# First norm's gain and shift applied behind the gather, in a decoder layer with 32 experts

## The chip, the cores and the metric

The kernel runs on one core of one Trainium2 chip. The metric is the device time of one execution in microseconds (us), as the median of several runs. A core has TensorE (PE, matmuls; its results go to PSUM), VectorE (DVE), ScalarE (ACT), GpSimd (POOL) and SyncE (SP), which here issues all the DMA transfers, in program order, each as soon as its buffer is free.

## The reference

One decoder layer of width 1024 over 512 tokens. Both norms are layer norms with a gain and a shift for each of the 1024 features:

```python
merged = gates[:, :, 0] * (pool_out @ w_pu[i]) + gates[:, :, 1] * (attn_out @ w_au[i])
x = layer_norm(DEEPNORM_ALPHA * x + merged @ w_o[i], ln1_g[i], ln1_b[i])
moe_out = hierarchical_moe(x, w_rg[i], b_rg[i], w_re[i], b_re[i], w_eg[i], w_eu[i], w_ed[i])
ple = jax.nn.sigmoid(x @ w_pg[i]) * (p[i] @ w_pp[i])
x = layer_norm(DEEPNORM_ALPHA * x + moe_out + ple, ln2_g[i], ln2_b[i])
```

`hierarchical_moe` sends each token to one of 4 groups by the largest of 4 logits and there to the two experts of 8 with the largest logits; an expert is `(silu(x @ w_eg) * (x @ w_eu)) @ w_ed` with 512 inner features. An expert's weights are 6 MB, those of all 32 together 192 MB.

## The kernel before

The tokens lie in four blocks of 128 rows (`tb` 0 to 3). Mixers and attention run first (to about 310 us); then comes `merged @ w_o` in two column halves (`out_proj`), and from its second half on everything around the change, in an order that is written out by hand (`tc.manual_schedule`); each engine works through its own instructions in that order.

**Norm and routing of a block.** `residual` adds alpha times the input and takes the statistics, `moments` and `shift` make the row's factor (with a power on GpSimd), `normalise` applies it on ScalarE (`acc[tb]` is then normalised, without gain and shift). `turn` transposes that into `x1T`, split into a high and a low part (ScalarE copies the high part out of PSUM, VectorE subtracts). `route` makes the logits from it; the gain and the shift are already folded into the router's weights and bias there. `gain`, `offset` and `affine` (L769 to L777) then multiply and add the rows of `ln1_g` and `ln1_b` into `acc[tb]`, each half on VectorE or GpSimd; `keep_high` (ScalarE) and `keep_low` (VectorE or GpSimd) split the result into the two parts of `x1[tb]`. `choose` picks group and experts for two blocks at a time in some 15 small VectorE instructions, `place` makes each token's slot with two or three matmuls, `one_hots` the matrix G that gathers.

**Gather and experts.** The 32 experts are worked on in 12 units of 2 to 4 experts; 128 slots are filled in each. `gather` multiplies x1 by G into PSUM, four banks `kb` 0 to 3 for the eight blocks of 128 features, and `keep_slots` copies them to `xgs`. For the first unit this goes bank by bank, blocks 0 and 1 of the tokens ahead, blocks 2 and 3 once the second choice is done; later units are gathered two at a time beside the experts, with the banks of `zz` (two). `inner` is the first pair of expert matmuls, `outer` the last one. The function `pair(j, ...)` runs one unit; between, `scatter` adds the unit before to `acc`. At the end of its first run `renew` (L894) rebuilds x1 from its two parts into `acc` on VectorE, scaled by alpha on ScalarE. Units 3 and 4 carry the first steps of `embedding`, which transposes x1 again (`split_transpose`) for `x @ w_pg`; it takes buffers out of the stream meanwhile.

**The weight stream.** Weights come in chunks of 1 MB, 192 in all. A chunk's buffer is one of 8 named s8, 6 of the pool wst (wraw, whi, wlo), 2 named more and, once each, 2 named acc. `FIRST` lists the chunks that go out before it is known which experts are busy (three experts are fixed, the rest go by a ranking of token counts that `count_tokens` and `rank` make); `eload_first(n)` issues them up to the nth. All others follow in their order through `eload_past`, each when TensorE has read a chunk and its buffer is free.

Of the kernel before, what the change touches and what calls it, by code (L numbers as in the profile page):

```python
# [20 lines left out]
S, D = 512, 1024  # L21
# [16 lines left out]
def layer_kernel(ctx: ExitStack, tc: tile.TileContext, x, p, w_in, w_pool, pool_scale, w_pu, w_au,  # L38
# [393 lines left out]

    x1, acc = {}, {}
# [16 lines left out]
    g1 = lnt.tile([128, D], F32, name="g1")  # L450
    b1 = lnt.tile([128, D], F32, name="b1")
    nc.sync.dma_start(g1, rows_bcast(ln1_g, D))
    nc.sync.dma_start(b1, rows_bcast(ln1_b, D))
# [60 lines left out]
    def source(i):  # L514
# [4 lines left out]
    FIRST = [(0, "s8"), (1, "s8"), (2, "s8"), (4, "s8"), (5, "wraw"), (6, "whi"), (8, "wlo"), (9, "wraw"), (10, "s8"),  # L519
             (11, "s8"), (12, "s8"), (15, "s8"), (18, "whi"), (21, "wlo"), (3, "acc"), (24, "more"), (27, "more"),  # L520
             (7, "acc")]
# [201 lines left out]
    def relabel(rk, w2):  # L723

        full = [128, 2, NT, E]
        t, u = (lnt.tile(full, F32, name=n, tag=t) for n, t in (("by_rank", "g1"), ("by_slot", "b1")))
# [42 lines left out]
    def gain(tb, h, eng):  # L769
        eng.tensor_mul(acc[tb][:, halves[h]], acc[tb][:, halves[h]], g1[:, halves[h]])  # L770

    def offset(tb, h, eng):
        eng.tensor_add(acc[tb][:, halves[h]], acc[tb][:, halves[h]], b1[:, halves[h]])

    def affine(tb, h, eng):
        gain(tb, h, eng)
        offset(tb, h, eng)  # L777

# [4 lines left out]
    def keep_high(tb):  # L783
        x1[tb] = res.tile([128, 2, D], F32R, name="x1", bufs=4)
        for h in range(2):
            nc.scalar.activation(turned(x1[tb][:, 0], h), acc[tb][:, halves[h]].rearrange("p (m k) -> p m k", k=KD), AF.Copy)
# [7 lines left out]
    eload_first(4)  # L794
# [25 lines left out]
    eload_first(8)  # L820
# [41 lines left out]
    def keep_slots(us, o, kb):  # L862
        o = o.rearrange("p (k e s) -> p k e s", k=2, e=2)
        ks = slice(2 * kb, 2 * kb + 2)
# [29 lines left out]
    def renew(b):  # L894

        new_acc(b)
        for tb in (b, b + 1):
            hi, lo = (x1[tb][:, i].rearrange("p (k m) -> p m k", k=KD).bitcast(F32) for i in range(2))
            nc.vector.tensor_add(acc[tb].rearrange("p (m k) -> p m k", k=KD), hi, lo)  # L899
# [12 lines left out]
    with tc.manual_schedule():  # L912
# [3 lines left out]
        eload_first(9)  # L916
# [8 lines left out]
        eload_first(10)  # L925
        residual(1, 1, o)
        moments(1)
        gain(0, 0, dve)
        shift(1)
        offset(0, 0, dve)  # L930
        affine(0, 1, pool)
# [87 lines left out]
    def pair(j, other, extra):  # L1019
# [19 lines left out]
        for n in range(2):  # L1039
# [14 lines left out]
            if n == 0:  # L1054
                embed(1)
# [330 lines left out]
```

## Time and profile before

| | us |
|---|---|
| median of 3 runs | 873.96 (873.03 to 874.01) |
| the profiled execution | 873.73 |
| its span in the trace | 871.9 |
| PE busy | 805.8 (92%) |
| DVE busy | 412.3 (47%) |
| ACT busy | 214.2 (25%) |
| POOL busy | 191.4 (22%) |

The trace is of one execution; its times count from the span's start. The DMA engines moved 241.89 MB in it, at 277 GB/s over the span; most of that is moved after 340 us. A busy PE need not be PE at its peak, since the ends of matmuls are modelled; whether it waits is read from who releases it, and whether the DMA engines are full from their mean share and rate.

### The profile page before, as it was taken

Reading aid. Unit: us, or ns where it says so; the run is one execution under the profiler, and the core shown is the slowest. Engines: PE = TensorE matmul, PEld = TensorE weight load, DVE = VectorE, ACT = ScalarE, POOL = GpSimd, SP = SyncE. Lnnn points to the kernel's source line nnn. Section 1 sums busy time; section 2 is a strip of 40 time slices with the busy share of each in tenths; the row PEclk is TensorE's granted clock in tenths of the full one; section 3 lists DMA queues with packets and bytes.
Section 4 is the critical chain, followed back from the end, with each engine's and each line's share of the span. In section 5 each row is a group of like instructions: output and inputs, shape, how many; then the busy total and the mean of one; then the engine's idle time right before and its main releaser. Section 6 shows DMA issues by size and latency. Waiting matters only on the chain.

```text
span 871.9 us, 11544 instructions
## 1 busy us (share of the span) xinstructions
PE 805.8 (92%) x4454; PEld 511.5 (59%) x4454; DVE 412.3 (47%) x691; ACT 214.2 (25%) x443; POOL 191.4 (22%) x176
## 2 busy tenths in 40 slices
PE   8999899899999998699999887899799999999983
PEld 7886677677768887635345333566375744545432
DVE  5278647645448858847442432221123244343437
ACT  3123444444461114313101011210220101100214
POOL 3333324224221235600000220231313000000225
PEclk9999999999999999689999989999999999999997
DMA  7431131222213786657999999999999999999992
GB/s 253 140 99 52 48 97 49 63 82 63 83 48 143 247 310 248 266 214 271 407 419 419 416 406 418 414 413 407 418 407 404 404 419 419 419 418 421 412 360 99
DMA packets 65787, 241.89 MB, mean 277 GB/s; under 512 B 12096, under 2 KB 32576, under 8 KB 41408
## 3 DMA queue, kind: packets, MB, share of 16 engines
q1 hardware_dynamic: 65728, 241.10, 71.1%
q8 instruction: 37, 0.61, 0.3%
q14 instruction: 22, 0.18, 0.1%
HBM read 238.99 MB, written 2.10 MB: 276 GB/s over the span
## 4 chain that ended last, share of the span: by engine, by line
PE 50%; DMA 11%; DVE 4%; POOL 2%; issue 1%; ACT 1%; SPq 1%; POOLq 0%; ACTq 0%; DVEq 0%
PE mm L907 18%; PE mm L1115 8%; PE xg_ps L848 6%; DMA ew<-in_w_eu_dram 4%; PE sc_ps L1148 4%; PE mm L143 3%; PE mm L145 3%; PE mm L144 3%; DMA ew<-in_w_ed_dram 3%; DMA pr<-in_p_dram 2%; DMA ew<-in_w_eg_dram 2%; PE pg_ps L144 1%; PE pg_ps L143 1%; PE pg_ps L145 1%; DVE acc L899 1%
## 5 line engine op out<-in xcount | busy, mean ns | idle before, releaser
L907 PE MATMUL mm<-ew,xg 128*32 128x512 f32 (+1 forms) x1088 | 189.5, 621 | 16.8 <-DMA ew<-in_w_eu_dram 11.1
L907 PEld LDWEIGHTS mm<-ew,xg 128*32 128x32 f32 (+1 forms) x1088 | 54.8, 125 | 137.3 <-issue 108.3
L1115 PE MATMUL mm<-ew,hT 128*32 128x512 f32 (+1 forms) x544 | 91.6, 597 | 3.0 <-DMA ew<-in_w_ed_dram 2.1
L132 POOL TENSOR_TENSOR wlo<-wraw,whi 128x1024 fp32r<-128x1024 f32 x23 | 69.1, 3003 | 108.4 <-DVE whi L127 52.5
L143 PE MATMUL mm<-xth,whi 128*128 128x512 f32 x224 | 91.6, 409 | 0.0
L145 PE MATMUL mm<-xth,wlo 128*128 128x512 f32 x224 | 88.6, 396 | 0.0
L144 PE MATMUL mm<-xtl,whi 128*128 128x512 f32 x224 | 88.3, 394 | 0.0
L1053 DVE TENSOR_TENSOR h<-mm,h 128x512 f32<-128x512 f32 x24 | 16.6, 692 | 128.9 <-PE mm L907 71.3
L848 PEld LDWEIGHTS xg_ps<-G,x 128*128 128x128 f32 x448 | 56.0, 198 | 13.6 <-issue 9.0
L848 PE MATMUL xg_ps<-G,x 128*128 128x256 f32 (+1 forms) x448 | 59.0, 290 | 1.2 <-DVE xg L867 1.2
L1149 DVE TENSOR_TENSOR acc<-acc,sc_ps 128x512 f32<-128x512 f32 x88 | 54.7, 681 | 6.6 <-PE sc_ps L1148 6.0
L1115 PEld LDWEIGHTS mm<-ew,hT 128*32 128x32 f32 (+1 forms) x544 | 24.7, 120 | 54.5 <-issue 46.1
L143 PEld LDWEIGHTS mm<-xth,whi 128*128 128x128 f32 x224 | 42.8, 191 | 9.5 <-issue 0.9
L144 PEld LDWEIGHTS mm<-xtl,whi 128*128 128x128 f32 x224 | 43.0, 192 | 8.8 <-issue 0.5
L145 PEld LDWEIGHTS mm<-xth,wlo 128*128 128x128 f32 x224 | 42.7, 190 | 9.3
L127 DVE CAST whi<-wraw 128x2048 fp32r<-128x2048 f32 x22 | 26.9, 1225 | 33.8 <-PE mm L144 16.6
L132 DVE TENSOR_TENSOR wlo<-wraw,whi 128x1024 fp32r<-128x1024 f32 x23 | 40.7, 1770 | 1.0
L1164 POOL TENSOR_TENSOR xf<-x 128x1024 f32<-128x1024 f32 x4 | 9.4, 2376 | 144.5 <-PE mm L907 144.5
L1137 POOL TENSOR_TENSOR accl<-acc,acch 128x512 fp32r<-128x512 f32 x8 | 10.5, 1337 | 137.7 <-ACT acch L1136 137.7
L1148 PE MATMUL sc_ps<-yh,Gt 128*128 128x512 f32 x88 | 37.8, 429 | 1.1 <-DVE sg L1220 1.1
L1220 DVE TENSOR_TENSOR sg<-pg_ps,sg 128x256 f32<-128x256 f32 x16 | 6.8, 425 | 65.4 <-ACT sg L1219 65.4
L144 PE MATMUL pg_ps<-pgl,xT 128*128 128x256 f32 x128 | 36.3, 284 | 0.7 <-POOL pgl L1200 0.7
(270 smaller groups left out, 1355.4 us busy)
## 6 DMA issues: line engine op xcount, KB each, us to landing
ew<-in_w_eg_dram SPq DMA_DIRECT2D x64, 1024.0 KB, 16.6
ew<-in_w_eu_dram SPq DMA_DIRECT2D x64, 1024.0 KB, 14.1
ew<-in_w_ed_dram SPq DMA_DIRECT2D x62, 1024.0 KB, 14.1
wraw<-in_w_in_dram SPq DMA_DIRECT2D x15, 1024.0 KB, 5.6
wraw<-in_w_o_dram SPq DMA_DIRECT2D x4, 1024.0 KB, 5.0
pgr<-in_w_pg_dram SPq DMA_DIRECT2D x4, 1024.0 KB, 17.3
wraw<-in_w_pu_dram SPq DMA_DIRECT2D x2, 1024.0 KB, 5.0
wraw<-in_w_au_dram SPq DMA_DIRECT2D x2, 1024.0 KB, 5.0
```

The source lines that it names most:

```text
L127: nc.vector.tensor_copy(hi, wraw[i])
L132: eng.tensor_sub(lo[:, j], wraw[i][:, j], hi[:, j].bitcast(F32))
L143: nc.tensor.matmul(o, lh, rh, start=start, stop=False)
L144: nc.tensor.matmul(o, lh, rl, start=False, stop=False)
L145: nc.tensor.matmul(o, ll, rh, start=False, stop=stop)
L848: nc.tensor.matmul(o[:, kx * 256:kx * 256 + n], x1[tb][:, i, cs], G[tb // 2][:, tb % 2].rearrange("p u s -> p (u s)"), start=whole and tb ...
L907: nc.tensor.matmul(o[cs], xgs[j][:, k, cs], ew[chunk0[j] + ne * (2 * n + k // 4) + i][:, k % 4], start=k == 0, stop=k == KD - 1)
L1053: nc.vector.tensor_mul(ht, o, ht)
L1115: nc.tensor.matmul(o[cs], hT[:, f, cs], ew[chunk0[j] + ne * (4 + f // 2) + i][:, f % 2, halves[c]], start=f == 0, stop=f == 3)
L1137: nc.gpsimd.tensor_sub(l, acc[tb][:, halves[c]], h.bitcast(F32))
L1148: nc.tensor.matmul(o, Gt[:, tb * 128:(tb + 1) * 128], y[c][i], start=i == 0, stop=i == 1)
L1149: nc.vector.tensor_add(acc[tb][:, cs], acc[tb][:, cs], o)
```

## The change

x1 is kept and gathered as normalised only. Gain and shift are applied three times later on: in `keep_slots`, where the gathered features lie one to a partition, so that gain and shift are columns `gq`, `bq` (ScalarE with scale and bias, VectorE with two scalars, one instruction for 128x128 where there was one for 128x256); in `renew`, a block at a time with the rows `gb1`; and in a new `turn_x1` for the embedding. `gain`, `offset` and `affine` go. `gb1` is an s8 buffer, which goes back to the stream at the end of the second pair; `FIRST` is one chunk shorter (27 is left out). `renew` runs for blocks 0 and 1 where it ran for all four, for block 2 at the end of the first pair and for block 3 inside the second.

```diff
+    gb1 = s8([128, 2, D], F32, "gb1")
+    gq, bq = (slp.tile([128, KD], F32, name=n) for n in ("gq", "bq"))
...
-             (11, "s8"), (12, "s8"), (15, "s8"), (18, "whi"), (21, "wlo"), (3, "acc"), (24, "more"), (27, "more"),
-             (7, "acc")]
+             (11, "s8"), (12, "s8"), (15, "whi"), (18, "wlo"), (3, "acc"), (21, "more"), (24, "more"), (7, "acc")]
...
-        nc.scalar.activation(xgs[us[0]][:, ks], o[:, :, 0], AF.Copy)
-        if len(us) > 1:
-            nc.vector.tensor_copy(xgs[us[1]][:, ks], o[:, :, 1])
+        for i in range(2):
+            k = 2 * kb + i
+            nc.scalar.activation(xgs[us[0]][:, k], o[:, i, 0], AF.Identity, scale=gq[:, k:k + 1], bias=bq[:, k:k + 1])
+            if len(us) > 1:
+                nc.vector.tensor_scalar(xgs[us[1]][:, k], o[:, i, 1], gq[:, k:k + 1], bq[:, k:k + 1], op0=OP.mult,
+                                        op1=OP.add)
...
+        nc.vector.tensor_add(acc[tb].rearrange("p (m k) -> p m k", k=KD), hi, lo)
+        nc.vector.tensor_mul(acc[tb], acc[tb], gb1[:, 0])
+        nc.vector.tensor_add(acc[tb], acc[tb], gb1[:, 1])
+        nc.scalar.activation(acc[tb], acc[tb], AF.Copy, scale=ALPHA)
...
-        turn(2, lambda: shift(3))
-        keep_low(1, 1, pool)
-        eload_first(15)
-        affine(2, 1, pool)
+        place(0)
+        turn(2)
+        keep_high(1, (0,))
+        shift(3)
         normalise(3)
-        place(0)
-        one_hots(G[0], (0,), 0)
-        gain(2, 0, dve)
...
         route(2)
+        keep_high(1, (1,))
+        keep_low(1, 0, pool)
+        keep_low(1, 1, dve)
+        one_hots(G[0], (0,), 0)
         turn(3)
-        offset(2, 0, dve)
-        affine(3, 0, dve)
-        affine(3, 1, pool)
+        keep_high(2)
+        keep_low(2, 0, pool)
         route(3)
...
-        for kb in range(3):
+        for kb in range(2):
             gather(G, xs[kb], kb, (0, 1))
-        keep_high(2)
         keep_high(3)
+        keep_low(2, 1, dve)
         choose(lg2, 2)
-        keep_low(2, 0, pool)
-        keep_low(2, 1, pool)
-        keep_low(3, 1, pool)
-        keep_low(3, 0, dve)
-        eload_first(18)
+        keep_low(3, 0, pool)
         place(2)
-        gather(G, xs[3], 3, (0, 1))
+        keep_low(3, 1, dve)
+        eload_first(17)
+        for kb in range(2, 4):
+            gather(G, xs[kb], kb, (0, 1))
...
+                if j == 1:
+                    renew(3)
...
-            for b in (0, 2):
-                renew(b)
+            renew(0)
+            renew(1)
...
+        if j == 0:
+            renew(2)
+        elif j == 1:
+            free.append("s8")
+            eload_past(done[0])
...
+        def turn_x1(xt, src):
+            for h in range(2):
+                pt = tt("x1T_ps")
+                t = ex.tile([128, 4, 128], F32, name="x1t", tag="pph", bufs=1)
...
+                    nc.vector.tensor_scalar(t[:, i], pt[:, i * 128:(i + 1) * 128], gq[:, k:k + 1], bq[:, k:k + 1],
+                                            op0=OP.mult, op1=OP.add)
+                hi, lo = (xt[:, i, 4 * h:4 * h + 4] for i in range(2))
+                nc.scalar.activation(hi, t, AF.Copy)
+                nc.vector.tensor_sub(lo, t, hi.bitcast(F32))
```

The order on VectorE from the first G to the beginning of the second choice, before (x1T are the transposed copies of block 3, g and b the gain and shift rows; `lg` is the choice's first instruction):

```order
L836 TENSOR_TENSOR G<-iota_c,posm 128x256
L770 TENSOR_TENSOR acc<-acc,g_2339 128x512
L596 TENSOR_TENSOR x1T<-x1T_ps,x1T 128x512 x2
L773 TENSOR_TENSOR acc<-acc,b_2340 128x512
L770 TENSOR_TENSOR acc<-acc,g_2339 128x512
L773 TENSOR_TENSOR acc<-acc,b_2340 128x512
L634 TENSOR_TENSOR lg<-lg_ps,lbias 128x80
```

The same stretch on VectorE after (x_2802 and x_2853 are x1 of blocks 1 and 2, so L782 is `keep_low`):

```order
L764 TENSOR_SCALAR rs<-mv,rs 128x1
L782 TENSOR_TENSOR x_2802<-acc,x_2802 128x64x8
L829 TENSOR_TENSOR G<-iota_c,posm 128x256
L598 TENSOR_TENSOR x1T<-x1T_ps,x1T 128x512 x2
L782 TENSOR_TENSOR x_2853<-acc,x_2853 128x64x8
L636 TENSOR_TENSOR lg<-lg_ps,lbias 128x80
```

Four steps with gain and shift are gone from in front of the choice, and two low parts of the split stand there.

On TensorE around the second placing, before (xg_ps with a number is a bank of the gather; 2826 is the fourth, 2823 the first again, for blocks 2 and 3):

```order
L659 MATMUL pos_ps_2952<-msk_2358,strict_67 128x64
L661 MATMUL pos_ps_2952<-msk_2358,ones_66 128x64 x2
L662 MATMUL pos_ps_2952<-msk_2358,ones_66 128x32
L848 MATMUL xg_ps_2826<-G_2544,x1_2688 128x128 x2
L848 MATMUL xg_ps_2826<-G_2544,x1_2742 128x128 x2
L848 MATMUL xg_ps_2826<-G_2544,x1_2688 128x128 x2
L848 MATMUL xg_ps_2826<-G_2544,x1_2742 128x128 x2
L670 MATMUL ct_ps_2968<-msk_2358,ones_66 128x32 x4
```

And after:

```order
L661 MATMUL pos_ps_2926<-msk_2361,strict_67 128x64
L663 MATMUL pos_ps_2926<-msk_2361,ones_66 128x64 x2
L664 MATMUL pos_ps_2926<-msk_2361,ones_66 128x32
L841 MATMUL xg_ps_2809<-G_2545,x1_2685 128x128 x2
L841 MATMUL xg_ps_2809<-G_2545,x1_2802 128x128 x2
L841 MATMUL xg_ps_2809<-G_2545,x1_2685 128x128 x2
L841 MATMUL xg_ps_2809<-G_2545,x1_2802 128x128 x2
L841 MATMUL xg_ps_2810<-G_2545,x1_2685 128x128 x2
L841 MATMUL xg_ps_2810<-G_2545,x1_2802 128x128 x2
L841 MATMUL xg_ps_2810<-G_2545,x1_2685 128x128 x2
L841 MATMUL xg_ps_2810<-G_2545,x1_2802 128x128 x2
L672 MATMUL ct_ps_2953<-msk_2361,ones_66 128x32 x4
```

The third bank's eight matmuls have moved from ahead of the placing to behind it.

On VectorE in the first pair, from the weights of its slots to the evictions of the next gather, before:

```order
L881 TENSOR_TENSOR Gw<-Gw,comb 128x512
L899 TENSOR_TENSOR acc<-x_2688 128x1024
L899 TENSOR_TENSOR acc<-x_2742 128x1024
L899 TENSOR_TENSOR acc<-x_2924 128x1024
L899 TENSOR_TENSOR acc<-x_2927 128x1024
L867 COPY xg<-xg_ps 128x256 x2
```

And after:

```order
L876 TENSOR_TENSOR Gw<-Gw,comb 128x512
L894 TENSOR_TENSOR acc<-x_2685 128x1024
L895 TENSOR_TENSOR acc<-acc,gb_2339 128x1024
L896 TENSOR_TENSOR acc<-acc,gb_2339 128x1024
L894 TENSOR_TENSOR acc<-x_2802 128x1024
L895 TENSOR_TENSOR acc<-acc,gb_2339 128x1024
L896 TENSOR_TENSOR acc<-acc,gb_2339 128x1024
L861 TENSOR_SCALAR xg<-xg_ps,gq,bq 128x128 x4
```

Two blocks instead of four are rebuilt there, each in three steps; the other two stand behind the pair's last results and inside the second pair.

## Rows read from the trace of the kernel before

**Rows 1.** Windows: engines' busy us (instructions), PE clock, DMA share, GB/s

```profile
760.00:800.00 40.00, 40.00 (x186) 16.94 (x184) 16.37 (x26) 3.76 (x6) 0.00 (x0) 1.00 1.01 419
```

**Rows 2.** Windows of 5 us at the stream's beginning

```profile
410.00:415.00 5.00, 5.00 (x52) 1.48 (x48) 1.82 (x3) 1.11 (x2) 0.00 (x0) 1.00 0.39 120
...
420.00:425.00 5.00, 5.00 (x39) 2.17 (x32) 1.48 (x3) 0.00 (x0) 0.00 (x0) 1.00 1.01 426
```

**Rows 3.** Chain that ended last, its end: start us, us, what

```profile
821.03 10.02 DMA ew<-in_w_eu_dram
...
835.35 8.43 DMA ew<-in_w_ed_dram
...
843.82 5.34 PE mm L1115 x42
```

**Rows 4.** Timeline of SP's queue: first issue behind the prefetched chunks

```profile
379.01 8.39 SPq L536 DMA_DIRECT2D ew<-in_w_eg_dram  x4
```

**Rows 5.** Chain from the second choice to the second pair

```profile
351.11 1.68 DVE acc L770
...
354.07 1.64 DVE acc L773
355.70 1.70 DVE acc L770
...
357.43 1.91 DVE acc L773
359.34 0.16 DVE lg L634
...
363.50 0.24 DVE msk L653
...
364.88 1.79 PE xg_ps L848 x8
...
371.93 3.61 PE mm L907 x8
...
377.11 1.87 PE mm L907 x8
...
409.53 13.87 PE mm L907 x128
```

**Rows 6.** Windows around TensorE's lower clock

```profile
360.00:370.00 10.00, 6.12 (x29) 6.15 (x30) 6.43 (x24) 1.84 (x3) 2.27 (x2) 0.50 0.45 164
...
376.00:378.00 2.00, 2.00 (x13) 1.36 (x14) 0.00 (x0) 0.38 (x1) 0.00 (x0) 0.84 0.00 0
```

**Rows 7.** Timeline of DVE: start us, us, line, operation, tiles

```profile
360.14 0.64 DVE L639 CAST gif<-gi 128x2 f32<-128x2 uint32 x1
...
361.96 1.12 DVE L649 CAST e<-i 128x4 f32<-128x4 uint32 x1
...
363.65 1.03 DVE L789 TENSOR_TENSOR x<-acc,x 128x512 fp32r<-128x512 f32 x1
```

**Rows 8.** Timeline of ACT: logits' copy and the high parts

```profile
351.08 0.27 ACT L613 ACTIVATE lt<-lg_ps 72x128 f32<-72x128 f32 x1
...
355.74 2.05 ACT L786 ACTIVATE x<-acc 128x512 fp32r<-128x512 f32 x2 [0.75 <-DVE acc L773]
```

**Rows 9.** Timeline of POOL: the last low part

```profile
361.53 1.52 POOL L789 TENSOR_TENSOR x<-acc,x 128x512 fp32r<-128x512 f32 x1 [0.79 <-ACT x L786]
```

**Rows 10.** Chain in the first pair: rebuild of x1 and eviction

```profile
393.96 9.68 DVE acc L899 x4
...
404.71 0.28 ACT xg L865
...
405.02 0.44 DVE xg L867
```

**Rows 11.** Groups by shape, 318 to 412 us: busy us, mean ns

```profile
L881 DVE TENSOR_TENSOR Gw<-Gw,comb 128x512 f32<-128x512 f32 x1 | 0.7, 691 | 0.0
```

**Rows 12.** Waits of PE from 420 to 860 us: us in total, times, longest

```profile
PE mm L907 <- DMA ew<-in_w_eu_dram: 11.1, 6, 5.1
```

More of the change, by code (lines that the diff above doesn't have):

```diff
@@ L449, in layer_kernel @@
         nc.sync.dma_start(acc[tb], x2[tb * 128:(tb + 1) * 128])
[L450 to L453, printed above, removed]
+    gb1 = s8([128, 2, D], F32, "gb1")
+    gq, bq = (slp.tile([128, KD], F32, name=n) for n in ("gq", "bq"))
+    for i, (w, t) in enumerate(((ln1_g, gq), (ln1_b, bq))):
+        nc.sync.dma_start(gb1[:, i], rows_bcast(w, D))
+        nc.sync.dma_start(t, w[0].rearrange("(p k) -> p k", p=128))
     wrr = lnt.tile([128, KD, 36], F32, name="wrr")
@@ L725, in relabel @@
         full = [128, 2, NT, E]
-        t, u = (lnt.tile(full, F32, name=n, tag=t) for n, t in (("by_rank", "g1"), ("by_slot", "b1")))
+        t, u = (lnt.tile(full, F32, name=n) for n in ("by_rank", "by_slot"))
         r2, s2 = (lnt.tile([128, 2, NT, 1], F32, name=n) for n in ("r2", "s2"))
@@ L767, in normalise, with keep_high @@
             nc.scalar.activation(acc[tb][:, cs], acc[tb][:, cs], AF.Identity, scale=rs[:, :1], bias=rs[:, 1:])
[L769 to L777, printed above, removed]
     def turned(t, h):
         return t.rearrange("p (k m) -> p m k", k=KD)[:, 64 * h:64 * h + 64]
-    def keep_high(tb):
-        x1[tb] = res.tile([128, 2, D], F32R, name="x1", bufs=4)
-        for h in range(2):
+    def keep_high(tb, hs=(0, 1)):
+        if 0 in hs:
+            x1[tb] = res.tile([128, 2, D], F32R, name="x1", bufs=4)
+        for h in hs:
             nc.scalar.activation(turned(x1[tb][:, 0], h), acc[tb][:, halves[h]].rearrange("p (m k) -> p m k", k=KD), AF.Copy)
@@ L892, in turn_one_hots, with renew @@
         return Gt, ws
[L894 to L899, printed above, removed]
+    def renew(tb):
+        if tb % 2 == 0:
+            new_acc(tb)
+        hi, lo = (x1[tb][:, i].rearrange("p (k m) -> p m k", k=KD).bitcast(F32) for i in range(2))
+        nc.vector.tensor_add(acc[tb].rearrange("p (m k) -> p m k", k=KD), hi, lo)
+        nc.vector.tensor_mul(acc[tb], acc[tb], gb1[:, 0])
+        nc.vector.tensor_add(acc[tb], acc[tb], gb1[:, 1])
+        nc.scalar.activation(acc[tb], acc[tb], AF.Copy, scale=ALPHA)
     def inner(j, n, o, ks):
@@ L924, in layer_kernel @@
         out_proj(1, 1, o, parts, range(6, 8))
-        eload_first(10)
+        eload_first(9)
         residual(1, 1, o)
         moments(1)
-        gain(0, 0, dve)
         shift(1)
-        offset(0, 0, dve)
-        affine(0, 1, pool)
         out_proj(2, 1, o, parts, range(0, 2))
@@ L943, in layer_kernel @@
         out_proj(2, 1, o, parts, range(6, 8))
-        eload_first(11)
+        eload_first(10)
         residual(2, 1, o)
         moments(2)
-        gain(1, 0, dve)
+        keep_low(0, 0, pool)
+        keep_low(0, 1, dve)
         shift(2)
-        offset(1, 0, dve)
-        affine(1, 1, pool)
         out_proj(3, 1, o, parts, range(0, 2))
@@ L1081, in pair @@
         if j == 0:
-            for b in (0, 2):
-                renew(b)
-                for tb in (b, b + 1):
-                    nc.scalar.activation(acc[tb], acc[tb], AF.Copy, scale=ALPHA)
+            renew(0)
+            renew(1)
         embed(3)
@@ L1109, in pair @@
         embed(5)
-        return Gt, [weighted(o[c], ws) for c in range(2)]
+        y = [weighted(o[c], ws) for c in range(2)]
+        if j == 0:
[3 more added lines that the diff above has]
+            eload_past(done[0])
+        return Gt, y
     def outer(j, hT, f, c, o):
@@ L1188, in embedding @@
             xT.append(xt)
-            split_transpose(xt, xf[tb])
+            turn_x1(xt, xf[tb])
             if tb % 2:
```

31 lines of the change are left out of this document (16 added, 15 removed).

## Prediction

> **What bounds the kernel now.** I read the stretches first, then the chain from its end backwards, then the SP queue. From 420 us the DMA engines are full: their share is 1.01, at 419 GB/s between 760 and 800 us [rows 1] and 426 at the start [rows 2], and the last two things that TensorE waits for are expert weights, 10.02 us and 8.43 us; the last weights land at 843.78 us and the rest is a fixed tail [rows 3]. So the end is set by the weight stream: by when it becomes full for good, and by how many chunks of 1 MB are still to come then. A chunk costs 1.0486 MB / 419 GB/s = 2.50 us.
>
> The stream could not be full earlier, for it had no free buffers. All 18 buffers are filled before the experts start; the first chunk behind them goes out at 379.01 us [rows 4], 0.03 us after TensorE has read the first chunks (377.11 + 1.87 us) [rows 5]. It stays so for the whole first pair: between 410 and 415 us the DMA share is still 0.39 [rows 2]. The second pair's 128 matmuls take 13.87 us from 409.53 us [rows 5] and free three chunks after each quarter of them, 3.5 us; the first three come free at 413.0 us. That is faster than 2.50 us a chunk can fill, and from there the stream has no gap. So two numbers decide: how much earlier TensorE gets to that point, and how many chunks are left at it.
>
> What TensorE waits for on the way is the second choice of experts. VectorE does four gain and offset steps in front of it (1.68, 1.64, 1.70 and 1.91 us), starts it at 359.34 us and ends it at 363.74 us; only then can TensorE place and gather [rows 5]. TensorE has been idle and is at half speed by then: eight matmuls of L907 take 3.61 us at 371.93 us and 1.87 us at 377.11 us [rows 5]; the granted clock is 0.50, the 1.2 GHz level, and comes back at about 376.7 us (0.84 over that stretch) [rows 6].
>
> **The change, part by part.**
>
> *One prefetch less.* gb1 takes one of the eight s8 buffers, so 17 chunks go out early and chunk 27 joins the stream. The buffer comes back only at the end of the second pair, when the stream is full anyway. Price: one chunk, **+2.50 us**. Its other loads cost nothing: the 1 MB of gain and shift rows stands where the second chunk stood, and the two 4 KB columns go out among the router's small loads. Chunk 3 now waits for VectorE as well as GpSimd before it may use the first acc buffer, and everything behind it on SP waits too (the two "more" chunks and chunk 7), but it is needed only near 376 us and is out some 20 us before that.
>
> *The choice comes earlier.* The four steps, 1.68 + 1.64 + 1.70 + 1.91 = 6.93 us, leave VectorE's queue. In their place stand two low parts of the split, on VectorE, at 1.03 us each when GpSimd is quiet [rows 7]: 6.93 - 2.06 = 4.87 us. I also walked the three queues in their new order with these durations, because the low parts wait for ScalarE's high parts (2.05 us a block [rows 8]), which now stand between the transposes and the logits. The walk's last steps: block 3's transposed copies leave ScalarE at 351.1 us, block 2's high parts 2.05 us later at 353.1, its low part leaves VectorE behind GpSimd's half at 354.7, and there the second choice starts, 4.7 us sooner. Its two casts can still be held up: the one at 361.96 us took 1.12 us and ended when GpSimd's subtraction of 361.53 + 1.52 us did [rows 7, 9]. Before, two casts lost about 1.4 us in this way; after it, one GpSimd subtraction (block 3) lies over the start of the choice, and one cast waits for it, about 0.9 us. So the choice ends 4.7 + 0.5 = **5.2 us** sooner, at 358.5 us. The bounds are 2.8 us (ScalarE's copies on the way, each late by the other) and 6.1 us (no hold-up).
>
> The Trainium skill (SBUF — State Buffer, section SBUF: two separate sides) says that VectorE and GpSimd share one port pair as an exclusive lock, which an instruction of VectorE with two SBUF inputs needs as well, and that the loser blocks fully. It speaks against the low parts on VectorE, and the trace agrees: the step at 357.43 us took 1.91 us beside GpSimd, against 1.03 us for a subtraction with GpSimd quiet. By that rule the low part of block 2 ends behind GpSimd's half, as in the walk; by the quiet row alone it would end 0.5 us sooner, and the sum would be -0.6 instead of -0.1 us.
>
> *Gather in another order.* Before, three of the four banks are gathered ahead of the second placing and one behind it; now two and two. So eight more matmuls stand behind the choice: 1.79 us at the half clock [rows 5], 0.9 us at full. I take **+1.79 us**, since the gathers do not bring the clock back (below). Net gain at the first expert matmul and at the first freed buffer: 5.2 - 1.8 = 3.4 us.
>
> *The first pair.* VectorE's rebuild of x1, four strided adds in 9.68 us [rows 10], stands in front of the eviction that TensorE waits for. Now it is two strided adds (2.42 each) and four steps of 128x1024 of which no row exists: 128x512 with two SBUF inputs takes 0.69 us [rows 11], so twice that, 1.38, is the upper near bound; taking off one instruction's fixed part I use 1.25. 2 x (2.42 + 2.50) plus hops = 10.0 us: +0.3 us (bounds -0.6 and +4.9, the latter if a plain step cost as much as a strided one). The eviction of a bank was one copy on ScalarE and one on VectorE, 0.28 + 0.44 us on the chain [rows 10]; it becomes four of 128x128 that take turns, since each waits for the other engine's last. The nearest row is 0.27 us for 72x128 [rows 8], the far bound the old 0.44: 4 x 0.27 + hops = 1.2 us, at most 1.8. So +0.5 us, and together **+0.8 us** (from -0.3 to +6).
>
> *What lies in cover.* The rebuild of blocks 2 and 3 (4.9 us each on VectorE, in the second pair) holds the product behind it by about 1 us; the scatter and the second half of that pair move back by as much. At that time twelve chunks have come free (four times three) and some four are filled (10.4 us / 2.50), so no transfer waits. Later evictions (0.4 us longer a bank) and turn_x1 (four more steps of some 0.27 us in each half block, 1.1 us, and one buffer x1t that holds the next half back) come where TensorE waits for weights: six waits of 11.1 us in all for one of the three weights alone [rows 12]. Without that cover turn_x1 would cost up to 8 x 1.2 = 9.6 us.
>
> **The sum.** -5.2 + 1.8 + 0.8 + 2.5 = -0.1 us, so against the profiled execution (873.73 us) **873.6 us**; that execution lies 0.23 us under the median of the three runs, 873.96. The routing's gain is real, but the lost prefetch eats it.
>
> **The rivals.**
>
> *The clock comes back sooner.* In the trace before, TensorE gathers without a pause from 364 to 372 us and stays at 0.50; it rises only 4.7 us after the first expert matmuls have begun. Before, it stood idle for most of the choice (6.12 us busy of the 10 from 360 us [rows 6]); now its first gathers end under 1 us before the placing, so it may be granted full speed from the second placing's first gather on. Some 14.5 us are at half clock in my sum; if all but the first 4.6 us go at full, (14.5 - 4.6) / 2 = 5 us are saved: 868.6 us. Against it: eight us of the same gathers did not do it before. The Trainium skill (TensorE: Matmul & The Clock Gate, What's actually happening) says that activity releases the throttle; by that rule the gathers before would have done so, and the trace does not agree for them.
>
> *The chunk is free.* If the weight stream had a gap later on, the lost prefetch would be made up there: 873.6 - 2.5 = 871.1 us. For it: TensorE is busy all the 40 us from 760 to 800 [rows 1]. Against it: the share is 1.01 there too, and the last two waits are for weights [rows 3].
>
> *ScalarE takes VectorE's place: slower.* The high parts of blocks 1 and 2 now stand ahead of block 3's transposed copies and its logits on ScalarE. If each of those is late by one copy of 1.03 us and the low part then collides with GpSimd, the second choice starts 2.4 us later than I say and ends 2.8 us sooner than before: -2.8 + 1.8 + 0.8 + 2.5 = +2.3, 876.0 us. It turns the sign for the measurement as soon as the choice gains less than about 3.3 us.
>
> *turn_x1 shows: slower.* The single x1t buffer makes the two halves of a block queue on VectorE and ScalarE, and scatter's adds stand behind them. If the chunks are then read so late that the stream runs dry, about half of the 9.6 us is paid: 878 us. It decides once TensorE's delay exceeds its waits for weights there.
>
> **How the numbers follow.** My forecast has 0.60, the clock 0.12, the free chunk 0.09, ScalarE 0.13, turn_x1 0.06. About 0.2% (1.75 us) is what a measurement of this kernel can tell from no change. Of the forecast's 0.60 the bounds of its terms put 0.13 under that line, 0.43 within it and 0.04 over. With the clock (0.12) and most of the free chunk (0.08) faster has 0.33; same 0.43 + 0.02 = 0.45; slower 0.04 + 0.12 + 0.06 = 0.22. Cases of both signs hold much of the chance; the likeliest one's own range is 871.3 to 875.6. The range of 870.0 to 876.5 takes in the free chunk and ScalarE and leaves out the clock and turn_x1, 0.18.
>
> **What would show it.** The second choice should end near 358.5 us, the first chunk behind the prefetched ones go out near 375.6 us, the stream become full for good near 410.4 us, and the last weights land within some us of 843.8 us, each 2.5 us off where the chunk comes in. A clock of 1.00 between 360 and 368 us would prove the second case. An end of the choice after 360.5 us would prove ScalarE's. DMA shares under 0.95 between 500 and 560 us would prove turn_x1's. The prediction is wrong in its base if the DMA share is well under 1 anywhere between 440 and 840 us.

## The result and the profile after

The changed kernel takes 878.82 us (median of 5 runs, 878.13 to 879.24), the kernel before on the same chip 873.96 us: a ratio of 1.006, 95% interval 1.0046 to 1.0075. So it is slower by about 5 us where 873.6 and no measurable difference had been forecast, and it lies above the range of 870.0 to 876.5. A second comparison, with a second profiled execution, gave 1.0055 (1.0042 to 1.0068). The profiled execution has a span of 877.1 us, before 871.9 us.

The second choice of experts, which the change was to bring forward, did come forward. The timeline of the changed kernel, VectorE and GpSimd (start us, us, engine, line, operation, out<-in, shape, count, and in brackets how long the engine had stood idle and for what; three dots stand for lines left out):

```profile
353.72 0.24 DVE L636 TENSOR_TENSOR lg<-lg_ps,lbias 128x80 f32<-128x80 f32 x1
...
354.01 1.54 POOL L782 TENSOR_TENSOR x<-acc,x 128x512 fp32r<-128x512 f32 x1 [1.16 <-ACT x L779]
...
354.61 0.96 DVE L641 CAST gif<-gi 128x2 f32<-128x2 uint32 x1
...
357.35 0.22 DVE L655 TENSOR_TENSOR msk<-oh 128x64 fp32r<-128x64 f32 x1
```

It starts at 353.72 us (before 359.34 [rows 5]) and ends at 357.57 us: 6.2 us earlier where 5.2 were forecast, with one cast of 0.96 us held until GpSimd's subtraction ends, as the walk of the queues had it. TensorE's own timeline shows what became of that gain:

```profile
372.92 3.68 PE L905 MATMUL mm<-ew,xg 128*64 128x512 f32 x8
376.53 1.11 PE L841 MATMUL xg_ps<-G,x 128*128 128x128 f32 x8
...
404.40 4.07 PE L841 MATMUL xg_ps<-G,x 128*128 128x256 f32 x32 [2.42 <-DVE xg L861]
```

The first expert matmuls start at 367.41 us, 4.5 us earlier. The second eight of them still run at the half clock (3.68 us; before 1.87 [rows 5]). Behind the rebuild TensorE waits 2.42 us for VectorE's eviction, where in the kernel before it had waited 1.23 us:

```profile
405.50 4.03 PE L848 MATMUL xg_ps<-G,x 128*128 128x256 f32 x32 [1.23 <-DVE xg L867]
```

The second pair starts at 408.4 us: of 4.5 us, 1.1 are left. In this execution some 2.1 us of the loss is the longer stretch at half clock, 1.3 us the way from the outer products to the gather. The windows of the changed kernel (TensorE, weight loads, VectorE, ScalarE and GpSimd busy, then clock, DMA share, GB/s):

```profile
360.00:370.00 10.00, 10.00 (x41) 7.99 (x42) 3.21 (x19) 1.61 (x4) 0.00 (x0) 0.50 0.43 159
410.00:415.00 5.00, 5.00 (x52) 1.56 (x48) 4.80 (x5) 1.06 (x2) 0.00 (x0) 1.00 0.38 100
565.00:570.00 5.00, 2.74 (x14) 2.74 (x15) 0.11 (x1) 0.00 (x0) 3.45 (x2) 0.76 0.71 263
590.00:595.00 5.00, 5.00 (x42) 1.60 (x34) 2.02 (x4) 1.51 (x2) 4.35 (x2) 1.00 0.85 308
```

The stretch from 410 us looks as it did before [rows 2]. New are the last two: the weight stream runs short at 565 and at 590 us, where before it was full:

```profile
565.00:570.00 5.00, 4.57 (x37) 4.13 (x35) 0.81 (x3) 0.77 (x2) 0.74 (x1) 1.00 1.07 372
590.00:595.00 5.00, 4.13 (x29) 1.38 (x30) 0.47 (x1) 0.00 (x0) 0.00 (x0) 1.00 1.02 419
```

Against a share of 1.01 the two windows lack an estimated 1.5 and 0.8 us of full stream. (The stream of the kernel before was not wholly without a gap either: its lowest share between 430 and 845 us is 0.92, at 655 us.) The last two waits for weights, from the changed kernel's chain:

```profile
826.61 10.14 DMA ew<-in_w_eu_dram
...
841.33 8.16 DMA ew<-in_w_ed_dram
```

The last weights land at 849.49 us, 5.7 us later than before [rows 3], and the tail behind them is about as long (27.6 us, before 28.1). The chain also says how the stream came to run dry:

```profile
542.14 4.05 PE xg_ps L841 x32
...
546.21 0.47 ACT xg L859
...
546.70 0.42 DVE xg L861
...
547.15 0.47 ACT xg L859
...
547.97 1.37 DVE x1t L1172 x4
...
549.38 0.66 PE gt_ps L882 x4
550.04 5.27 PE mm L1110 x32
555.30 4.04 PE xg_ps L841 x32
...
559.37 0.47 ACT xg L859
...
559.87 0.42 DVE xg L861
...
560.67 1.91 ACT pgh L1210
...
562.71 4.51 POOL pgl L1211
```

ScalarE and VectorE empty a bank in turn; the new turn of x1 follows on VectorE; TensorE meanwhile waits 2.33 us (before 0.98), falls to half clock (32 matmuls in 5.27 us, elsewhere 3.57), gathers later, and ScalarE's split pgh comes only behind the last bank's evictions, 1.33 us after the gather's end. GpSimd's pgl and the embedding's products that need it are late in turn, with TensorE's expert products, and so the buffers, behind them. In the chain of the kernel before, pgh starts 0.30 us behind the gather's end:

```profile
550.88 3.95 PE xg_ps L848 x32
...
555.13 1.91 ACT pgh L1199
```

### The profile page after: what moved, and what is told of

Same layout as the page of the kernel before. It is cut to its first block, busy times and chain, and to the rows that moved or that the text cites. A ratio compares the mean times of both kernels' runs of the same rounds, so it can differ in the third digit from the quotient of the medians.

```text
span 877.1 us, 11632 instructions
## 1 busy us (share of the span) xinstructions
PE 812.8 (93%) x4454; PEld 515.6 (59%) x4454; DVE 429.1 (49%) x746; ACT 228.4 (26%) x471; POOL 174.5 (20%) x165
## 4 chain that ended last, share of the span: by engine, by line
PE 29%; DMA 18%; DVE 2%; issue 2%; POOL 1%; ACT 1%; SPq 1%; POOLq 0%; DVEq 0%; ACTq 0%
PE mm L905 11%; DMA ew<-in_w_eu_dram 8%; PE mm L1110 7%; DMA ew<-in_w_eg_dram 4%; PE xg_ps L841 4%; DMA ew<-in_w_ed_dram 3%; PE sc_ps L1143 3%; DMA pr<-in_p_dram 2%; PE pg_ps L143 1%; PE pg_ps L144 1%; PE pg_ps L145 1%; POOL pgl L1211 1%; SPq L538 0%; PE hT_ps L1057 0%; PE gt_ps L882 0%
## 5 line engine op out<-in xcount | busy, mean ns | idle before, releaser
L841 PEld LDWEIGHTS xg_ps<-G,x 128*128 128x128 f32 x448 | 59.6, 207 | 15.5 <-issue 12.3
L841 PE MATMUL xg_ps<-G,x 128*128 128x256 f32 (+1 forms) x448 | 62.6, 300 | 2.4 <-DVE xg L861 2.4
L859 ACT ACTIVATE xg<-xg_ps,bq,gq 128x128 f32<-128x128 f32 x56 | 24.7, 456 | 89.2 <-PE xg_ps L841 79.5
```

The source lines that it names most:

```text
L841: nc.tensor.matmul(o[:, kx * 256:kx * 256 + n], x1[tb][:, i, cs], G[tb // 2][:, tb % 2].rearrange("p u s -> p (u s)"), start=whole and tb ...
L859: nc.scalar.activation(xgs[us[0]][:, k], o[:, i, 0], AF.Identity, scale=gq[:, k:k + 1], bias=bq[:, k:k + 1])
```

## The experiments

The prediction's sum has four terms that could be wrong: the chunk, the evictions, the turn of x1, the order of the gathers. Each got a kernel.

**Without the new turn of x1.**

```
-            turn_x1(xt, xf[tb])
+            split_transpose(xt, xf[tb])
```

> The changed kernel with turn_x1 replaced by the turn that the kernel before used there, split_transpose: no gain and shift on the embedding's rows, so the product x @ w_pg is computed from the normalised rows alone; everything else as in the changed kernel. Theory A (the new turn of x1 lengthens the embedding's chain, the second load of pgr holds eight expert loads behind it on SP's queue, and the weight stream runs dry between 560 and 600): the DMA engines stay above 0.95 in every slice of 5 us from 520 to 620, the last weights land about 4.3 us earlier, and the time is about 874.5 us. Rival B (the time was lost before 420, by the routing, the clock and the chunk that is no longer prefetched, and the dry stretch only shows a loss that the stream would have had anyway): 878.8 us, within 0.5.

Measured: 877.59 us, ratio 1.0051 (1.0035 to 1.0067). The stream still ran dry (0.74 at 565 us). By the ratios the new turn costs 0.4 to 0.8 us, which the intervals don't separate from nothing; theory A in this form fell.

**The embedding's load later on SP's queue.**

```
-            if q < 3:
-                raw = load(q + 1)
             yield
             for tb in range(NT):
+                if tb == 1 and q < 3:
+                    raw = load(q + 1)
```

> The changed kernel with turn_x1 kept, but the load of the next quarter of w_pg placed one block of tokens later in the program, so that on SP's queue it stands behind the expert loads that waited for it. Theory A1 (the loss between 560 and 600 is SP's queue held up by one load whose buffer POOL has not yet left): no slice of 5 us from 550 to 600 under 0.95 DMA, and about 875 us. Rival A2 (the turn's own latency on the way from DVE to PE costs the time, through the expert products that come later behind it): the DMA share still falls, and the time stays at 878 to 879 us.

Measured: 877.86 us, 1.0058 (1.0045 to 1.0071). The gap at 565 us went (1.01), another came at 580 (0.78) and 590 us (0.73). So SP's queue passes the delay on but doesn't cause it. That the buffers themselves come free late is how I read the chain above; this run alone does not show it.

**Evictions as before the change.**

```
+        ks = slice(2 * kb, 2 * kb + 2)
+        nc.scalar.activation(xgs[us[0]][:, ks], o[:, :, 0], AF.Copy)
+        if len(us) > 1:
+            nc.vector.tensor_copy(xgs[us[1]][:, ks], o[:, :, 1])
```

> The changed kernel with the evictions of the gathered rows as in the kernel before, one copy of 128x256 for each expert and bank instead of two with scale and shift: gain and shift are left out of the experts' inputs. Theory (the evictions' doubled count costs 0.4 to 0.8 us at each pair's gather, and 1 us where the embedding meets the third pair): second pair's first product about 407.6 instead of 408.4, pgl about 1 us earlier, time 877 to 878 us. Rival (evictions lie beside the stream and cost nothing): 878.8 us, within 0.4.

Measured: 871.07 us, 0.9985 (0.9972 to 0.9998), for a kernel that leaves gain and shift out of the experts' inputs. I had expected 1 us and it was over 6: everything that the kernel had lost, and more. TensorE's timeline, with a wait of 1.39 us and the second pair from 404.65 us:

```profile
400.62 4.10 PE L841 MATMUL xg_ps<-G,x 128*128 128x256 f32 x32 [1.39 <-DVE xg L860]
404.65 13.94 PE L903 MATMUL mm<-ew,xg 128*32 128x512 f32 x128
```

**The missing chunk alone.** The kernel before with 17 chunks prefetched. In a first version GpSimd was the held buffer's only reader, had no reason to wait, and the eighteenth chunk went into it at 371.68 us:

```
+    idle = s8([128, 2, D], F32, "idle")
+    nc.sync.dma_start(idle[:, 0, :4], rows_bcast(ln1_g, 4))
...
+        if j == 1:
+            nc.gpsimd.tensor_copy(idle[:1, 1, :4], idle[:1, 0, :4])
+            free.append("s8")
```

> The kernel before with one chunk less prefetched: 17 instead of 18, the same list as in the changed kernel, and the freed buffer of 8 KB held until the end of the second pair. Nothing of the norm, the routing or the gather is touched. Theory (a chunk that isn't prefetched is a chunk more in a stream that is full from 413 to 844): last weights land 2.5 us later, time 876.5 us. Rival (the stream has slack in the first pairs and the chunk is free): 874.0 us, within 0.4.

Measured: 873.22 us, 1.0002 (0.9994 to 1.0011), which shows only that a chunk loaded at 371 instead of 365 us costs nothing. In a second version the buffer is held by VectorE into the second pair:

```
+                if j == 1:
+                    nc.vector.tensor_add(idle[:1, 1, :4], idle[:1, 0, :4], h[:1, :4])
```

> The kernel before with 17 chunks prefetched instead of 18 and the buffer of 8 KB held until VectorE has read it in the first half of the second pair, as the changed kernel holds gb1 (in the earlier run of this kind the buffer's only reader came too soon, and the eighteenth chunk was loaded at 371 into it). Theory (a chunk that can't be loaded before the stream is full costs its 2.5 us): last weights 2.5 us later than before, 875.5 us against 873.0. Rival (the chunk is free): 873.0, within 0.4.

Measured: 875.06 us, 1.0023 (1.0015 to 1.0032), so 2.0 us; in its chain the last weights land at 845.70 us, 1.9 us later than before:

```profile
837.54 8.16 DMA ew<-in_w_ed_dram
```

The chunk isn't free, and its price (1.3 to 2.8 us by the interval) is near the 2.5 us of the sum.

**The changed kernel once more**, for a second profile:

> The changed kernel itself, unchanged, for a second profiled execution beside the runs that follow. In the first one TensorE's clock came back to full at about 376 us; in three kernels that differ from it only behind 400 us it came back near 371. Theory (the return differs from one execution to the next and is paid back later: where it comes early, the wait of 2.4 us before the second pair's gather costs a second drop near 401, as it did in the run with the old turn): the time is again 878 to 879 us, within 0.2%, whichever way the clock goes. Rival (the return is fixed by the code and the other three were faster by it): return at 376 again.

Measured: 877.99 us, ratio 1.0055. The clock came back at 372 us (in the first profile at about 376.5), and was lost again behind the wait near 400 us, so that the same 32 matmuls of the gather took 5.56 instead of 4.07 us:

```profile
402.14 5.56 PE L841 MATMUL xg_ps<-G,x 128*128 128x256 f32 x32 [2.41 <-DVE xg L861]
```

**Evictions dealt out by banks.** If not the number of operations but the taking of turns costs the time, the same operations in another division must give it back:

```
-            nc.scalar.activation(xgs[us[0]][:, k], o[:, i, 0], AF.Identity, scale=gq[:, k:k + 1], bias=bq[:, k:k + 1])
-            if len(us) > 1:
-                nc.vector.tensor_scalar(xgs[us[1]][:, k], o[:, i, 1], gq[:, k:k + 1], bq[:, k:k + 1], op0=OP.mult,
-                                        op1=OP.add)
+            for e, j in enumerate(us):
+                if kb % 2 and len(us) > 1:
+                    nc.vector.tensor_scalar(xgs[j][:, k], o[:, i, e], gq[:, k:k + 1], bq[:, k:k + 1], op0=OP.mult,
+                                            op1=OP.add)
+                else:
+                    nc.scalar.activation(xgs[j][:, k], o[:, i, e], AF.Identity, scale=gq[:, k:k + 1],
+                                         bias=bq[:, k:k + 1])
```

> The changed kernel, complete, with the eviction of the gathered rows dealt out by banks instead of by experts: ScalarE takes both experts of an even bank (four operations of 128x128), VectorE those of an odd one, so that no bank waits for both engines in turn. Same operations, same count. Theory (the loss is the bank that ScalarE and VectorE empty in turn, step behind step, first at the first pair, where VectorE comes to it only after the rebuild, and again at the third pair): TensorE waits under 0.5 us before the second pair's gather instead of 2.4, no drop of the clock at 401 or 550, no dry stretch of the stream at 565, time 871 to 874 us. Rival (it is the engines' time in itself, 0.44 and 0.41 us each, that is too much): 877 to 879 us.

Measured: 872.48 us, 0.9985 (0.9975 to 0.9995), with the whole computation done: 6.1 us less than the changed kernel, and as fast as with the old evictions. What taking turns means is to be seen in the changed kernel's timeline of the first pair:

```profile
402.43 0.44 ACT L859 ACTIVATE xg<-xg_ps,bq,gq 128x128 f32<-128x128 f32 x1
402.91 0.41 DVE L861 TENSOR_SCALAR xg<-xg_ps,gq,bq 128x128 f32<-128x128 f32 x1 [1.47 <-ACT xg L859]
403.35 0.81 ACT L859 ACTIVATE xg<-xg_ps,bq,gq 128x128 f32<-128x128 f32 x2 [0.48 <-DVE xg L861]
403.85 0.76 DVE L861 TENSOR_SCALAR xg<-xg_ps,gq,bq 128x128 f32<-128x128 f32 x2 [0.53 <-ACT xg L859]
```

Each engine stands idle for about 0.5 us between its steps while the other works on the same bank. By banks, four such steps run on one engine without a gap, and ScalarE begins its bank at 400.34 us, 0.29 us before VectorE has ended the other:

```profile
399.27 1.36 DVE L861 TENSOR_SCALAR xg<-xg_ps,gq,bq 128x128 f32<-128x128 f32 x4
...
400.34 1.49 ACT L864 ACTIVATE xg<-xg_ps,bq,gq 128x128 f32<-128x128 f32 x4
...
400.77 2.99 PE L841 MATMUL xg_ps<-G,x 128*128 128x256 f32 x23 [0.88 <-DVE xg L861]
```

The Trainium skill (PSUM — Partial Sum Buffer, Terms) says that two engines may not be on one bank at once, reads included; so a program has to let them take turns there. The two blocks of rows agree with it: in turn on one bank, for 0.29 us at the same time on two. What becomes of two engines on one bank at once no run here shows.

**One loss or two?** Against the kernel by banks: only the gather of units 1 and 2 (near 400 us) is dealt out by banks and all later ones by experts, or, with `us[0] > 1` in the same place, only the later ones by banks:

```
-                if kb % 2 and len(us) > 1:
+                if len(us) > 1 and (kb % 2 if us[0] == 1 else e):
```

> The changed kernel with the eviction dealt out by banks only at the first gather behind the placing (the one of units 1 and 2, near 400 us), and by experts, as in the changed kernel, at all later ones. By banks everywhere gave 6.1 us. Theory A (two separate losses: TensorE's wait and the drop of the clock near 401, some 2.5 us, and the stream that runs dry near 565, some 3.6 us, from the later gather's evictions): 875.5 us, with the dry stretch still there. Rival B (one loss: the stream runs dry only because the second unit started late): 872 to 873 us, no dry stretch.

> The complement: by experts at the first gather near 400 us, by banks at all later ones. Theory A: 874.5 us, with TensorE's wait of 2.4 us near 400 still there and no dry stretch near 565. Rival B: 878 us, the dry stretch still there.

Measured: 875.53 us, 1.0025 (1.0016 to 1.0035), and 874.36 us, 1.0017 (1.0008 to 1.0026). Against 1.0055 that is 2.6 and 3.3 us, each within about 1.4 us, together 5.9 of 6.1. Counted from the other end, against 0.9985 of the kernel by banks, it is 2.8 us for the first gather and 3.5 for the later ones. So there are two losses. The windows near 565 and at 590 us, first of the kernel with only the first gather by banks,

```profile
560.00:565.00 5.00, 2.15 (x10) 2.16 (x11) 0.70 (x2) 0.00 (x0) 4.03 (x2) 0.80 0.88 350
...
590.00:595.00 5.00, 4.32 (x32) 0.92 (x29) 0.81 (x2) 0.00 (x0) 2.55 (x2) 1.00 0.92 346
```

then of the one with only the later ones:

```profile
565.00:570.00 5.00, 4.98 (x41) 4.98 (x42) 0.42 (x1) 0.39 (x1) 1.51 (x2) 1.00 0.92 326
...
590.00:595.00 5.00, 3.54 (x21) 0.87 (x23) 1.29 (x2) 0.00 (x0) 3.19 (x2) 1.00 1.01 416
```

In the first the stream still has its gaps (0.88 and 0.92), in the second one small one is left (0.92) and that at 590 us is gone. The second trace is of an execution of 877.34 us, 3 us over its median, and has one more window under 0.90 behind, 0.81 at 820 us. The clock alone does not make the gaps: in the first kernel it stayed at full at 547 us behind a wait of 2.34 us (32 matmuls in 3.64 us), in the second TensorE fell to half clock at 549 us (5.27 us). What differs is pgh. In the second kernel's chain ScalarE, which has no part of the last bank, begins it before the gather ends:

```profile
554.85 2.12 PE xg_ps L841 x16
...
557.35 1.15 ACT xg L864 x3
558.50 1.81 ACT pgh L1213
```

The last gather's 32 matmuls end near 558.9 us, and pgh starts at 558.50 instead of 1.33 us behind.

**The evictions' form in the kernel before.** Two copies of 128x128 for each of 128x256, nothing else:

```
-        nc.scalar.activation(xgs[us[0]][:, ks], o[:, :, 0], AF.Copy)
-        if len(us) > 1:
-            nc.vector.tensor_copy(xgs[us[1]][:, ks], o[:, :, 1])
+        for i in range(2):
+            k = 2 * kb + i
+            nc.scalar.activation(xgs[us[0]][:, k], o[:, i, 0], AF.Copy)
+            if len(us) > 1:
+                nc.vector.tensor_copy(xgs[us[1]][:, k], o[:, i, 1])
```

> The kernel before with nothing of the change but the form of its evictions: two copies of 128x128 for each expert and bank, one k after the other, as in the changed kernel, and still dealt out by experts. Theory (the engines that empty one bank in turn, in smaller steps, cost the 6 us by themselves): 878 to 879 us, with a wait of 2.4 us before the second pair's gather and a dry stretch of the stream near 565. Rival (they cost only beside the rebuild and the new turn of x1, which come with the rest of the change): under 875 us.

Measured: 873.58 us, 1.0008 (0.9997 to 1.002). By itself the form cost 0.7 us, which the interval (up to 1.7 us) doesn't part from nothing: TensorE's two waits became 1.48 and 1.34 us, the clock stayed at full behind both, and no window from 430 to 845 us has a share under 0.92.

```profile
405.42 3.97 PE L848 MATMUL xg_ps<-G,x 128*128 128x256 f32 x32 [1.48 <-DVE xg L869]
```

The theory that it costs 6 us anywhere fell. But the steps here are plain copies of 0.28 and 0.29 us, against 0.44 to 0.46 and 0.41 us with gain and shift. No run has the short steps in the changed kernel, so how much of the 6 us is the number of steps and how much their length is not parted.

**By banks in the kernel before:**

```
+        for e, j in enumerate(us):
+            if kb % 2 and len(us) > 1:
+                nc.vector.tensor_copy(xgs[j][:, ks], o[:, :, e])
+            else:
+                nc.scalar.activation(xgs[j][:, ks], o[:, :, e], AF.Copy)
```

> The kernel before with the gathered rows' eviction dealt out by banks: ScalarE empties even banks (two copies of 128x256), VectorE odd ones. Theory (the wait of 1.23 us for VectorE before the second pair's gather bounds the kernel before as well): the wait falls to nothing, the second pair starts 1.2 us earlier, 871.8 us against 873.0. Rival (the start of the second pair isn't what fills the stream): 873.0, within 0.4.

Measured: 872.88 us, 0.9994 (0.9986 to 1.0003): no measurable gain. The wait only fell from 1.23 to 0.89 us and ended with ScalarE's eviction now; ScalarE's scaling of the rebuilt block stands ahead of it in its queue.

**Scaling once.** That queue position, in the changed kernel with its evictions by banks: gain and shift are multiplied by ALPHA once, and the four scalings of ScalarE go.

```
+        for i in range(2):
+            nc.scalar.activation(gb1[:, i], gb1[:, i], AF.Copy, scale=ALPHA)
...
-        nc.scalar.activation(acc[tb], acc[tb], AF.Copy, scale=ALPHA)
```

> The changed kernel with the eviction dealt out by banks, and gain and shift multiplied by ALPHA once (two operations of ScalarE behind the second placing), so that the four rebuilds need no scaling on ScalarE any more. In the run with banks alone ScalarE's two operations of 1.06 us on the rebuilt blocks stood ahead of its evictions, and TensorE still waited 0.88 us before the second pair's gather. Theory (that queue position is what is left of the wait): the wait falls to nothing, the second pair starts 0.9 us earlier, 871.6 us against 872.5 with the banks alone and 873.1 before. Rival (other engines decide the start of the stream by now): 872.5, within 0.4.

Measured: 869.52 us, 0.9966 (0.9949 to 0.9984). TensorE goes from the outer products to the gather without a wait, for ScalarE's evictions now run from 396.23 us beside VectorE's rebuild:

```profile
398.48 3.65 PE L1114 MATMUL mm<-ew,hT 128*64 128x512 f32 x16
402.07 4.10 PE L841 MATMUL xg_ps<-G,x 128*128 128x256 f32 x32
```

By the ratios of 0.9985 and 0.9966 it gave 1.7 us (3.0 us by the medians) over the banks alone, but the two intervals overlap. Its seven runs fall in two groups, four from 868.0 to 869.5 us and three from 872.8 to 873.9; the trace is of one of the slower (873.88 us). The slower three have the lower mean granted clock (0.959 to 0.962, the others 0.964 to 0.968); why stays open. So the wait is shown to be gone, and what that is worth is not.

**Rebuild on GpSimd** of blocks 2 and 3, to have gb1's buffer back early, beside the two edits above:

```
-            renew(0)
-            renew(1)
+            renew(2, nc.gpsimd)
+            renew(0)
+            renew(1)
+            renew(3, nc.gpsimd)
...
         if j == 0:
-            renew(2)
-        elif j == 1:
             free.append("s8")
```

> As the kernel with banks and scaled gain, with blocks 2 and 3 rebuilt by POOL beside VectorE's blocks 0 and 1 in the first pair (POOL has nothing else to do from 360 to 465), so that gb1's buffer comes free at the end of the first pair instead of the second. Theory (the buffer then takes its chunk while the stream still has gaps, and the 2.0 us of the missing chunk come back): 869.5 us. Rival (POOL's three operations a block, 1.3 to 2.4 us each for 512 to 1024 columns, slow VectorE's own rebuild, and the second pair starts later): 873 to 876 us.

Measured: 879.77 us, 1.008 (1.0067 to 1.0093): the rival, and worse. The timeline:

```profile
385.89 2.41 POOL L898 TENSOR_TENSOR acc<-acc,gb 128x1024 f32<-128x1024 f32 x1
386.13 2.45 DVE L739 TENSOR_TENSOR by_slot<-by_rank,s 128x256 f32<-128x256 f32 x1
...
399.41 1.09 PE L1059 MATMUL hT_ps<-ident,h 128*128 128x128 f32 x4 [10.94 <-issue]
```

The step of VectorE shown, 0.43 us in the changed kernel, took 2.45 and ended 0.28 us behind the operation of GpSimd beside it; four more small steps of the routing went the same way (0.29 to 0.43 us became 2.3 to 3.7), and TensorE stood for 10.94 us. That is 10 us more than with the same rebuild on VectorE, for a chunk of 2.

**Three banks ahead of the placing**, beside the evictions by banks:

```
-        for kb in range(2):
+        for kb in range(3):
             gather(G, xs[kb], kb, (0, 1))
...
-        for kb in range(2, 4):
-            gather(G, xs[kb], kb, (0, 1))
+        gather(G, xs[3], 3, (0, 1))
```

> The changed kernel with the eviction dealt out by banks and with three banks of the gather instead of two ahead of the second placing, as before the change. Theory (the prediction's term: eight matmuls less behind the placing, 1.79 us at half the clock, of which the placing itself gives back what TensorE then ends its third bank late, 1.1 us by the row of the changed kernel): first products 0.7 us earlier, 871.8 us. Rival (without effect, or slower because the clock then falls or returns at another time): 872.5 us and above.

Measured: 871.27 us, 0.9974 (0.9962 to 0.9986), 1.0 us less than with the banks alone by the ratios, with intervals that overlap. The first products start at 366.62 us, 0.9 us earlier than there.

**All that helped**, banks, scaling and three banks ahead in one kernel:

> All that helped, together: eviction by banks, gain and shift scaled once, three banks of the gather ahead of the second placing. Alone beside the banks they gave 1.2 us (three banks) and 3.0 us (scaling). Theory (both move the start of the second unit, one by earlier products, one by a shorter wait, so they add): 868.5 us. Rival (TensorE, no longer held, meets the next limit, or the clock returns later): 869.5 to 871 us.

Measured: 869.35 us, 0.9956 (0.9942 to 0.997), the fastest by ratio, 3.8 us under the kernel before and over 8 under the changed one. Its interval lies clear of that of the banks alone (0.9975 to 0.9995); from the scaling beside the banks (0.9966) it does not part it.

## Why the prediction was wrong, point by point

- **The bound** was right: the weight stream sets the end, and nothing behind it changed. That it has no gap from the second pair on was not quite so even before (0.92 at 655 us), and in the changed kernel the prediction's own sign of a wrong base is there, a share of 0.71 at 565 us.
- **The choice, -5.2 us**: right, 6.2 us, beyond the upper bound by 0.1. (Over all profiles its end lies from 356.2 to 357.9 us with the change and from 362.5 to 363.9 without.) The gathers' new order, +1.79, was right too: from the choice's end to the first product it is 9.84 us, before 8.14. So with 5.2 us the first products should have come 3.4 us earlier, and with 6.2 they came 4.5. Three banks ahead give back only 0.9 us of it, since the placing itself then starts 0.8 us later (358.67 instead of 357.83 us).
- **The clock sooner**, a rival: 0.50 all through 360 to 370 us in both executions. It did not come. In one execution of two the first pair's start was even at half clock for longer than in the sum, since the second eight products were too.
- **The chunk, +2.50 us**: right in sign and nearly in size, 2.0 us by the run with the held buffer. The rival that it is free fell.
- **The first pair, +0.8 us: the step that failed first.** The rebuild was right (9.87 us against 10.0). The eviction was mis-sized: I took 0.27 us a step from the row of a 72x128 copy and had 0.44 us as the far end. For a plain copy that is right (0.28 us in the run with halves in the kernel before), but with gain and shift the steps took 0.44 to 0.46 us on ScalarE and 0.41 on VectorE. Four of them in turn put 1.1 us instead of 0.5 between the rebuild and the gather (2.96 us, before 1.86), and I had no term for what a longer wait does to the clock: in the second execution the gather behind it ran at half clock, another 1.5 us. By the run with only this gather dealt out by banks it is 2.6 us.
- **Later evictions and turn_x1 "lie in cover": the step that failed most.** I counted waits for weights as room for all of it. But near 541 us the evictions, the turn and the split pgh stand in one chain between TensorE's gathers, and at its end hang the buffers that the stream needs. A bank's eviction there takes 1.84 us where it took 0.84, so 1.0 us longer and not 0.4. By the run with only the later gathers by banks the evictions cost 3.3 us; turn_x1 itself is 0.4 to 0.8 us.
- **The rival turn_x1**, with 0.06, had the right place, the right consequence (the stream runs dry) and nearly the right time (878 us), but the wrong cause: with the old turn the gap was still there. Its marker, a share under 0.95 between 500 and 560 us, looked a little too early; the gap begins at 565 us.
- **ScalarE takes VectorE's place**: the choice ended before 358 us; it did not happen.

The sum by what the runs and the trace show: -4.5 (first products, trace; in the trace of the kernel by banks the second pair is 4.7 us earlier than before) + 2.0 (chunk) + 6.1 (evictions by experts) + 0.4 to 0.8 (turn) = +4.0 to +4.4 us, measured +4.8. The difference is smaller than what the intervals of these terms can tell.

## What to carry to other kernels

When a cheap operation between TensorE and a buffer is split in two, ask first whether its halves can run beside each other: here two engines that shared a PSUM bank took turns, two that had a bank each didn't, and dealing out whole banks was worth 6 us of 874. Part of that came from a side effect, ScalarE's being free of the last bank and so starting pgh earlier. Cover is a property of a place, not of a stretch: waits for weights a few microseconds away don't hide a chain on which the release of the next buffers hangs. And for a wait of TensorE that grows by 1 us the slower clock that may follow it belongs in the sum.

## What the runs showed of the hardware

- The same wait of TensorE went either way for its clock: after 2.42 us near 402 us the clock stayed at full in the first profile of the changed kernel (a gather in 4.07 us), after 2.41 us it was at the 1.2 GHz level in the second (5.56 us). After the waits of 1.39, 1.48 and 0.91 us there it stayed at full. Of the five profiles with a wait of 2.4 to 2.5 us at that place, the three in which the clock had come back before 373 us lost it (5.55 to 5.57 us for the gather), and the two in which it had come back at about 376 us kept it (4.07 us).
- When the clock comes back differs by 4.5 us between two executions of the changed kernel (372 and about 376.5 us), and the time did not follow: 878.95 and 878.82 us, since the earlier return was followed by the loss near 402 us.
- Beside an operation of GpSimd a step of VectorE with two inputs from SBUF took about as long as that operation, five times in a row: 2.45 us for a step of 0.43 in the rows above. The Trainium skill (SBUF — State Buffer, section SBUF: two separate sides) describes a lock that does this, and the trace agrees.
